# Chain outputs turned by VectorE, and small transfers issued by GpSimd, in a hybrid layer

## The chip, the cores and the metric

The kernel runs on one core of a Trainium2 chip. The engines of that core are TensorE (PE, matrix products and transposes; PEld is its weight load), VectorE (DVE), ScalarE (ACT), GpSimd (POOL) and SyncE (SP); 16 DMA engines move data between memory and the core. An engine that issues a transfer does so in its own instruction queue. The metric is the device time of one execution in microseconds (us), taken as the median of several runs.

## The reference

One layer of a decoder trunk on `x` of 1024 tokens by 1024 channels, in float32. The input projection feeds two mixers, whose outputs are concatenated and projected back; then comes a gated MLP with a short convolution. Cut to what matters:

```python
h = rmsnorm(x, norm1_w)
proj = h @ w_in
# mixer A: 4 heads of 128, chunked delta rule
o_a = gated_delta_rule(qa, ka, va, g, beta)
o_a = rmsnorm(o_a, gdn_norm_w) * silu(z)
# mixer B: 8 heads of 64, three dilated windows merged by their denominators
num_tot = wts[0] * nums[0] + wts[1] * nums[1] + wts[2] * nums[2]
den_tot = wts[0] * dens[0] + wts[1] * dens[1] + wts[2] * dens[2]
o_b = num_tot / den_tot
x = x + concatenate([o_a, o_b]) @ w_out
u = causal_dwconv(rmsnorm(x, norm2_w) @ w_up, ffn_conv_w)
x = x + (silu(u[..., :D_FF]) * u[..., D_FF:]) @ w_down
out = rmsnorm(x, final_norm_w)
```

## The kernel before

Activations are kept channel-major (128 channels by 1024 tokens a tile). A float32 product is three passes over high and low halves (`xhi`·`whi`, `xlo`·`whi`, `xhi`·`wlo`), called a product of three passes here. The input projection runs column by column in the order of the list `DENSE`: the last key column, the values of the attention, the q and v columns of the delta-rule heads, eight attention columns `a`, and four gate columns `z`. Weights are fetched two columns ahead by `take`; for the last twelve columns (`a`, `z`) ScalarE makes the high half `whi` and GpSimd the low half `wlo` (L225).

The delta rule of head h is `chain(h)`: eight chunks of 128 tokens, one after the other. Heads 0 and 1 run ahead of heads 2 and 3. At its end GpSimd takes a power (`ms`) and scales the token-major output `vtok` by it, and `finish(h, vtok)` (L926) turns that output to channel-major. Heads 0 and 1 are turned by TensorE (`tp`, eight transposes each), copied with the factor `gw2` by ScalarE to a tile `ot`, and written by SP to `mixer`. Heads 2 and 3 are turned by VectorE, whose transpose works inside blocks of 32 by 32, and the blocks are put in place by eight writes to `odram`, 512 runs of 32 numbers each. A gate column `z` reads the head's output back as `og` (one transfer from `mixer`, or four from `odram`) and multiplies it with the gate.

The attention begins when the outputs of all four heads are written (`wv.until(("o", h))`). It takes eight groups (four pairs of heads, two halves of the tokens). In a group, each pair of blocks goes through `scores`, `softmax`, `turn` (TensorE transposes the weights, VectorE and ScalarE copy them to `pt` and `pb`), and `values`; `merge_classes` adds the dilated part. For groups 0 to 6 `rows_out` brings the reciprocals of the denominators across partitions: VectorE turns them (`dt`), four transfers of 1 KB write them to `ddram`, two transfers read them, repeated over 64 partitions, as `rT`. `give` (L1101) multiplies the accumulator with `rT` to `oT`, and frees one of two accumulator banks. `ot`, `rT` and `oT` share a ring `t2` of two buffers. The factors of the second norm take a similar way in `rms2_power`: four writes to `ndram` and one read, `rstdB`.

The order of TensorE's work is set by a planner (`Weave`) that runs the parts of the program as streams with priorities and keeps an estimate of each engine's time; the order it finds is fixed for TensorE by a token (`mm` L194, `tp` L198). The other engines' order is made by a scheduler after that, and each executes its queue in order. The object that issues is an `Engine` (L142, L144); `sy` and `sq` are two names of SP's queue with different costs for the planner, and `sq` issues the small transfers: the writes `odram`, the reads `og` from it, `ddram`, `rT` and `ndram`.

Of the kernel before, what the change touches and what calls it, by code (L numbers as in the profile page):

```python
# [7 lines left out]
F32 = mybir.dt.float32  # L8
F32R = mybir.dt.float32r
AF = mybir.ActivationFunctionType  # L10
OP = mybir.AluOpType
# [4 lines left out]
P = 128  # L16
# [3 lines left out]
NCH = 8  # L20
# [127 lines left out]
def hybrid_layer(tc, I, out):  # L148
    nc = tc.nc
    wv = Weave()  # L150
    ve = Engine(wv, nc.vector, "vector", 0.07, 0.00105)
    ac = Engine(wv, nc.scalar, "scalar", 0.12, 0.00085)
# [2 lines left out]
    ua = Engine(wv, nc.scalar, "scalar", 0.12, 0.00085, first=tc.high_priority)  # L155
    po_ = Engine(wv, nc.gpsimd, "gpsimd", 0.15, 0.0021)
    sy = Engine(wv, nc.sync, "sync", 0.05, 0.00142, 2.2)
    sq = Engine(wv, nc.sync, "small", 0.05, 0.00036, 0.4)
    sa = Engine(wv, nc.scalar, "actq", 0.05, 0.00142, 2.2)
    es = ExitStack()  # L160
    cp = es.enter_context(tc.tile_pool(name="cp", bufs=1))
# [2 lines left out]
    sp = es.enter_context(tc.tile_pool(name="sp", bufs=1))  # L164
# [3 lines left out]
    def tile_(pool, shape, dt, name, tag, bufs):  # L168
        return wv.slot(pool.tile(list(shape), dt, name=name, tag=tag, bufs=bufs), tag, bufs)
# [3 lines left out]
    def A(name, tag, dt=F32, shape=(P, 1024)):  # L173
        if tag in TURNS:
            i = turns[tag] = turns.get(tag, -1) + 1
            tag = TURNS[tag][i % len(TURNS[tag])]
        return tile_(lp, shape, dt, name, tag, SLOTS[tag])
# [4 lines left out]
    def const(name, shape, src=None):  # L182
        t = cp.tile(list(shape), F32, name=name)
        if src is not None:
            sy.dma_start(t, src)
        return t
# [10 lines left out]
    def tp(dst, src, idt=None, us=0.11):  # L197
        tc.stamp_issue_order_token(nc.tensor.transpose(dst, src, ident if idt is None else idt).ins, TOKEN)  # L198
        wv.product(us, dst, src)
# [13 lines left out]
    def raw_weight(src, n=1024):  # L213
        st = tile_(wp, [P, n], F32, "wst", "wst", 2)
        sy.dma_start(st, src)
        return st
# [37 lines left out]
    mixer = dp.tile([8, P, S], F32, name="mixer")  # L254
# [10 lines left out]
    odram = dp.tile([H, 32, 4 * S], F32, name="odram")  # L265
# [3 lines left out]
    def bank(tag, name="ps"):  # L269
        return tile_(pp_, (P, 512), F32, name, tag, 2)  # L270

    def next_bank(tag, *tiles, slack=0.0):

        while max(wv.need(*tiles), wv.slot_free(tag, 2)) + slack > 1e-3:
            yield max(wv.need(*tiles), wv.slot_free(tag, 2)) + slack
        return bank(tag)

    def half(i):
        return slice(i * 512, i * 512 + 512)

    def v8(t):
        return t.rearrange("p (c t) -> p c t", c=NCH)
# [83 lines left out]
    gw2 = const("gw2", [P, 1])  # L366
# [149 lines left out]
    def silu2(xr, name):  # L516
        y = A(name, "ev")
        ac.activation(y, xr, AF.Tanh, scale=0.5)
        ve.scalar_tensor_tensor(y, y, 1.0, xr, op0=OP.add, op1=OP.mult)
        return y  # L520
# [8 lines left out]
    def first_keys():  # L529
        xr = [scaled(pst[2 * h:2 * h + 2], "xr", tag=("ev", "ev", "qa")[h]) for h in range(3)]  # L530
        for h in range(3):
            T["k", h] = conv_silu(xr[h], 4 + h, "kT", "kT*")
            wv.add(3, kprep(h))
            yield wv.need(T["k", h])

    def dense():

        yield from wv.until("first")
        yield from wv.until("norms")
        wv.add(2, first_keys())  # L540

        srcs, tiles = [], 0
        for col in DENSE:
            if col[0] == "V":
                srcs += [I["wv"][j] for j in range(4)]
            else:
                srcs.append(I["wi"][tiles])
                tiles += 1
        place = [0]
        raw = [raw_weight(srcs[0])]  # L550
        nxt = [weight(None, st=raw.pop())]
        raw.append(raw_weight(srcs[1]))

        def take():
            w = nxt.pop()
            i = place[0] = place[0] + 1
            if i < len(srcs):
                nxt.append(weight(None, st=raw.pop(), spare=i >= 17))
            if i + 1 < len(srcs):
                raw.append(raw_weight(srcs[i + 1]))  # L560
            return w

        def values_by_token(g):

            banks = [bank(t) for t in ("asc", "asc", "ch", "ch")]
            for j in range(4):
                w = [t.rearrange("p (k m) -> p k m", k=2) for t in take()]
                for kk in range(2):
                    k = 2 * j + kk
                    for i, pt in enumerate(banks):  # L570
                        c = 4 * g + i
                        yield wv.need(pt, *w)
                        mm3(pt, [t[:, c * P:(c + 1) * P] for t in xs[k]], [t[:, kk, :] for t in w], k == 0, k == KT - 1)
            for i in range(0, 4, 2):
                vx = A("vx", "ev", shape=(P, 2, 512))
                for e in range(2):
                    c = 4 * g + i + e
                    ac.activation(vx[:, e, :], banks[i + e], AF.Copy, scale=rst[:, c:c + 1])
                c = 4 * g + i
                sy.dma_start(vpark[c * P:(c + 2) * P].rearrange("(e p) d -> p e d", e=2), vx)  # L580
            wv.done.add(("V", g))

        for i, col in enumerate(DENSE):
            kind, h = col[:2]
            if kind == "V":
                yield from values_by_token(h)
                continue
            if kind == "z":
                yield from wv.until(("o", h))
            w = [t.rearrange("p (k m) -> p k m", k=KT) for t in take()]  # L590
            pair = []
            for hh in range(2):
                pt = bank("hf")
                yield wv.need(pt, *w)
                for k in range(KT):
                    mm3(pt, [t[:, k, :] for t in w], [t[:, half(hh)] for t in xs[k]], k == 0, k == KT - 1)
                    yield 0.0

                pair.append(pt)
                if hh == 0:  # L600
                    xr = A("aqkv" if kind == "a" else "xr", "go" if kind == "k" else "ev")
                scaled(pair, "xr", kind == "a", t=xr, hs=(hh,))
            if kind == "k":
                T["k", h] = conv_silu(xr, 4 + h, "kT", "kT*")
                wv.add(3, kprep(h))
            elif kind == "q":
                q = conv_silu(xr, h, "qT", "qa")
                wv.add(4, qprep(h, q))
            elif kind == "v":
                v = conv_silu(xr, 8 + h, "vT", "qa")  # L610
                wv.add(4, vprep(h, v))
            elif kind == "z":
                og = gated[h] = A("og", "kT*")
                if h > 1:
                    of = odram[h].rearrange("j (c a t) -> a j c t", c=NCH, a=4)
                    for a in range(4):
                        sq.dma_start(v8(og)[32 * a:32 * a + 32], of[a])
                else:
                    sy.dma_start(og, mixer[h])
                zz = silu2(xr, "zz")  # L620
                if h > 1:
                    ve.scalar_tensor_tensor(og, og, gw2, zz, op0=OP.mult, op1=OP.mult)
                else:
                    ve.tensor_tensor(og, og, zz, op=OP.mult)
            else:
                sy.dma_start(apark[h, col[2]], xr)
                wv.done.add(col)
        wv.done.add("dense")
# [295 lines left out]
        wv.add(1, finish(h, vtok))  # L924

    def finish(h, osb):  # L926
        if h > 1:
            yield wv.need(osb)
            for hh in range(2):
                ot = tile_(sp, [P, 512], F32, "ot", "t2", 2)  # L930
                for c in range(4):
                    ve.transpose(ot[:, c * P:c * P + P], osb[:, (4 * hh + c) * P:(4 * hh + c + 1) * P])
                to = odram[h].rearrange("j (f b i) -> b j f i", f=32, b=4)[:, :, 16 * hh:16 * hh + 16]
                for b in range(4):
                    sq.dma_start(to[b], ot[32 * b:32 * b + 32].rearrange("p (f i) -> p f i", i=32))
        for hh in range(2 * (h < 2)):
            pt = yield from next_bank("atr", osb)
            for c in range(4):
                i = 4 * hh + c
                tp(pt[:, c * P:(c + 1) * P], osb[:, i * P:(i + 1) * P])  # L940
            ot = tile_(sp, [P, 512], F32, "ot", "t2", 2)
            ac.activation(ot, pt, AF.Copy, scale=gw2)
            sy.dma_start(mixer[h][:, half(hh)], ot)
        wv.done.add(("o", h))


# [797 lines left out]
```

## Time and profile before

| what | us |
| --- | --- |
| median of 3 runs | 1196.23 (1195.36 to 1197.35) |
| the profiled execution, its time | 1197.55 |
| the profiled execution, its span | 1195.7 |
| TensorE busy in it | 1182.3 |
| VectorE busy | 918.3 |
| ScalarE busy | 569.5 |
| GpSimd busy | 81.5 |

The clock granted to TensorE was 0.998 of full speed over the span. All rows quoted from the profile come from the one profiled execution, and their times count from the start of its span. A row of a timeline gives start, duration, engine, line, operation, output and inputs, and in brackets how long the engine stood idle before it and what ended that. L142, L144, L194 and L198 are lines of helpers, so that rows are told apart by the names of tiles.

### The profile page before, as it was taken

To read this page: it belongs to the slowest core of one execution; us is meant where nothing else is said; L and a number is where in the kernel's file an instruction comes from. 1 tells how busy PE (TensorE), PEld (TensorE's weight loads), DVE (VectorE), ACT (ScalarE), POOL (GpSimd) and SP (SyncE) were. 2 spreads that over 40 slices of the span, in tenths; PEclk is the share of its full clock that TensorE was granted. 3 is DMA by queue.
4 is the path that set the end of the run, shared out by engine and by line. 5 is a ranking of instruction groups with operands and counts; after the bars stand their busy time and mean duration, and the time that the engine had idled before them with its cause. 6 is when DMAs were issued, how large, how long until landed. Compare 5 with 4: busy or idle time off the path is not lost.

```text
span 1195.7 us, 18260 instructions
## 1 busy us (share of the span) xinstructions
PE 1182.3 (99%) x6998; PEld 977.3 (82%) x6998; DVE 918.3 (77%) x1473; ACT 569.5 (48%) x1115; POOL 81.5 (7%) x74
## 2 busy tenths in 40 slices
PE   9999999999999999999999999999999999999997
PEld 7888888888777778888888888888888888887886
DVE  7673975666365665777898898989889889998875
ACT  7275345355354533555554444445444453434441
POOL 0212010214211110000000000000000000000000
PEclk9999999999999999999999999999999999999999
DMA  7334234435944214443322313132231397546514
GB/s 244 101 95 150 80 116 127 143 122 172 220 147 129 86 52 135 159 159 106 106 86 73 106 53 106 54 106 81 78 103 56 127 368 284 197 160 211 168 53 141
DMA packets 100023, 157.20 MB, mean 131 GB/s; under 512 B 30400, under 2 KB 51168, under 8 KB 99936
## 3 DMA queue, kind: packets, MB, share of 16 engines
q1 hardware_dynamic: 99072, 155.25, 40.1%
q8 instruction: 55, 0.90, 0.3%
q10 hardware_dynamic: 864, 0.79, 0.2%
q14 instruction: 32, 0.26, 0.1%
HBM read 120.04 MB, written 35.96 MB: 130 GB/s over the span
## 4 chain that ended last, share of the span: by engine, by line
PE 93%; DVE 3%; ACT 2%; issue 1%; DMA 1%; POOLq 0%; POOL 0%; DVEq 0%; SPq 0%; ACTq 0%
PE ps L194 45%; PE pa L194 20%; PE dw L194 15%; PE pc L194 10%; PE ps L198 2%; DVE kT L142 1%; DMA wd<-in_wd 1%; DVE x1h L142 0%; ACT sm L144 0%; DVE pr L142 0%; DMA xt<-in_xT 0%; ACT whi L142 0%; DVE zz L142 0%; DVE wd L142 0%; ACT dec L142 0%
## 5 line engine op out<-in xcount | busy, mean ns | idle before, releaser
L194 PE MATMUL dw<-pr 128*128 128x512 f32 (+1 forms) x984 | 212.0, 377 | 0.3 <-DVE x1h L142 0.2
L194 PEld LDWEIGHTS dw<-pr 128*128 128x128 f32 x984 | 176.6, 188 | 34.7 <-DVE x1h L142 1.2
L194 PE MATMUL ps<-xhi,whi 128*128 128x512 f32 x384 | 157.1, 409 | 0.1
L194 PE MATMUL ps<-xhi,wlo 128*128 128x512 f32 x384 | 150.1, 391 | 0.0
L194 PE MATMUL ps<-xlo,whi 128*128 128x512 f32 x384 | 148.3, 390 | 0.0
L194 PE MATMUL pa<-T,pair 128*128 128x512 f32 x528 | 127.1, 389 | 0.1
L194 PEld LDWEIGHTS pa<-T,pair 128*128 128x128 f32 x528 | 99.0, 188 | 20.9 <-ACT u L142 0.5
L194 PEld LDWEIGHTS ps<-xhi,whi 128*128 128x128 f32 x384 | 72.3, 188 | 19.1 <-issue 5.6
L194 PEld LDWEIGHTS ps<-xhi,wlo 128*128 128x128 f32 x384 | 72.2, 188 | 15.6
L194 PEld LDWEIGHTS ps<-xlo,whi 128*128 128x128 f32 x384 | 72.3, 188 | 12.6
L142 ACT ACTIVATE u<-pa 128x512 f32<-128x512 f32 x44 | 26.3, 598 | 108.7 <-PE pa L194 108.7
L142 DVE SCALAR_TENSOR_TENSOR y<-xu,fcw,y 128x1023 f32<-128x1023 f32 (+1 forms) x44 | 56.4, 1281 | 23.3 <-ACT y L142 23.2
L142 ACT ACTIVATE whi<-wst 128x1024 fp32r<-128x1024 f32 x36 | 38.2, 1065 | 63.6 <-PE ps L194 45.9
L194 PE MATMUL pa<-B,A 128*128 128x512 f32 x264 | 63.4, 389 | 0.0
L194 PE MATMUL pc<-T,S 128*128 128x512 f32 x264 | 63.4, 389 | 0.0
L194 PE MATMUL pa<-T,S 128*128 128x512 f32 x264 | 63.4, 389 | 0.0
L194 PE MATMUL pc<-B,pair 128*128 128x512 f32 x264 | 63.4, 389 | 0.0
L142 ACT ACTIVATE pr<-r 128x1024 fp32r<-128x1024 f32 (+1 forms) x44 | 36.6, 840 | 51.8 <-PE dw L194 29.5
L142 DVE TENSOR_TENSOR wst<-wst 128x512 f32<-128x512 f32 x88 | 60.4, 687 | 0.8
L194 PE MATMUL ps<-B,pair 128*128 128x512 f32 x252 | 60.5, 389 | 0.0
L194 PEld LDWEIGHTS pa<-T,S 128*128 128x128 f32 x264 | 49.6, 188 | 10.3
L194 PEld LDWEIGHTS pc<-B,pair 128*128 128x128 f32 x264 | 49.6, 188 | 10.3
(255 smaller groups left out, 2322.5 us busy)
## 6 DMA issues: line engine op xcount, KB each, us to landing
wst<-in_wu SPq DMA_DIRECT2D x44, 512.0 KB
wd<-in_wd SPq DMA_DIRECT2D x44, 512.0 KB
upark<-y SPq DMA_DIRECT2D x22, 512.0 KB
wst<-in_wi SPq DMA_DIRECT2D x21, 512.0 KB
r<-upark SPq DMA_DIRECT2D x11, 512.0 KB
r<-upark SPq DMA_DIRECT2D x22, 256.0 KB
wa<-in_wd SPq DMA_DIRECT2D x22, 256.0 KB
wst<-in_wv SPq DMA_DIRECT2D x8, 512.0 KB
```

The lines of the kernel that those rows point to most:

```text
L142: return getattr(eng, op)(*a, **kw)
L194: tc.stamp_issue_order_token(nc.tensor.matmul(dst, lhs, rhs, start=start, stop=stop, **kw).ins, TOKEN)
L198: tc.stamp_issue_order_token(nc.tensor.transpose(dst, src, ident if idt is None else idt).ins, TOKEN)
```

## The change

The name `sq` now stands for GpSimd's queue. `finish` does one thing for all heads: its stream waits until the planner has placed the last chunks of chains 2 and 3, then VectorE turns the output and eight transfers of `sq` write it to `odram`. The gate columns read every head by four transfers of `sq` and always apply `gw2`.

```diff
-    sq = Engine(wv, nc.sync, "small", 0.05, 0.00036, 0.4)
+    sq = Engine(wv, nc.gpsimd, "small", 0.05, 0.00036, 0.4)
...
             elif kind == "z":
                 og = gated[h] = A("og", "kT*")
-                if h > 1:
-                    of = odram[h].rearrange("j (c a t) -> a j c t", c=NCH, a=4)
-                    for a in range(4):
-                        sq.dma_start(v8(og)[32 * a:32 * a + 32], of[a])
-                else:
-                    sy.dma_start(og, mixer[h])
-                zz = silu2(xr, "zz")
-                if h > 1:
-                    ve.scalar_tensor_tensor(og, og, gw2, zz, op0=OP.mult, op1=OP.mult)
-                else:
-                    ve.tensor_tensor(og, og, zz, op=OP.mult)
+                of = odram[h].rearrange("j (c a t) -> a j c t", c=NCH, a=4)
+                for a in range(4):
+                    sq.dma_start(v8(og)[32 * a:32 * a + 32], of[a])
+                ve.scalar_tensor_tensor(og, og, gw2, silu2(xr, "zz"), op0=OP.mult, op1=OP.mult)
...
     def finish(h, osb):
-        if h > 1:
-            yield wv.need(osb)
-            for hh in range(2):
-                ot = tile_(sp, [P, 512], F32, "ot", "t2", 2)
-                for c in range(4):
-                    ve.transpose(ot[:, c * P:c * P + P], osb[:, (4 * hh + c) * P:(4 * hh + c + 1) * P])
-                to = odram[h].rearrange("j (f b i) -> b j f i", f=32, b=4)[:, :, 16 * hh:16 * hh + 16]
-                for b in range(4):
-                    sq.dma_start(to[b], ot[32 * b:32 * b + 32].rearrange("p (f i) -> p f i", i=32))
-        for hh in range(2 * (h < 2)):
-            pt = yield from next_bank("atr", osb)
+        for i in (2, 3):
+            yield from wv.until(("c", i, NCH - 1))
+        yield wv.need(osb)
+        for hh in range(2):
+            yield 0.3
+            ot = tile_(sp, [P, 512], F32, "ot", "t2", 2)
             for c in range(4):
-                i = 4 * hh + c
-                tp(pt[:, c * P:(c + 1) * P], osb[:, i * P:(i + 1) * P])
-            ot = tile_(sp, [P, 512], F32, "ot", "t2", 2)
-            ac.activation(ot, pt, AF.Copy, scale=gw2)
-            sy.dma_start(mixer[h][:, half(hh)], ot)
+                ve.transpose(ot[:, c * P:c * P + P], osb[:, (4 * hh + c) * P:(4 * hh + c + 1) * P])
+            to = odram[h].rearrange("j (f b i) -> b j f i", f=32, b=4)[:, :, 16 * hh:16 * hh + 16]
+            for b in range(4):
+                sq.dma_start(to[b], ot[32 * b:32 * b + 32].rearrange("p (f i) -> p f i", i=32))
         wv.done.add(("o", h))
```

Three places show how the order of instructions moves. The first is TensorE among the last chunks of the chains: the difference from before (-) to after (+), where head 0 was turned. `xhi`, `wlo` belong to the input projection; `wke`, `ktok`, `r`, `um` to the chains.

```order
 L194 MATMUL ps<-xlo,whi 128x512
 L194 MATMUL ps<-xhi,wlo 128x512
-L198 MATMUL ps<-ident,vtok 128x128 x8
-L194 MATMUL ps<-wke,ktok 128x128
-L194 MATMUL ps<-r,um 128x128
```

The eight transposes of head 0 are gone (and two times four of head 1, a little later); products of the projection and the chains are interleaved anew around that place. Of the products of three passes that stood ahead of the turn of attention group 4, four now stand earlier, ahead of group 2.

The second place is GpSimd from the end of chain 0 on, difference from before to after. `ms` is the power at the end of a chain, `vtok` the scaled output, `pb` a cleared tile of the attention.

```order
 L142 TENSOR_TENSOR ms<-ms,mhalf 128x8
+L142 DMA odram<-ot 32x16x32
 L142 TENSOR_TENSOR vtok<-vtok,ms 128x1024
+L142 DMA odram<-ot 32x16x32 x7
 L142 MEMSET pb 32x2x128
 L142 TENSOR_TENSOR ms<-ms,mhalf 128x8
+L142 TENSOR_TENSOR wlo<-wst,whi 128x1024
 L142 TENSOR_TENSOR vtok<-vtok,ms 128x1024
-L142 TENSOR_TENSOR wlo<-wst,whi 128x1024
+L142 DMA odram<-ot 32x16x32 x8
 L142 MEMSET pb 32x2x128
```

The writes of heads 0 and 1 now stand between the powers, the scaled outputs and the low halves of GpSimd's own work. Further down the same queue after the change, from the small writes of attention group 1 to the reads of group 2:

```order
 L142 DMA ddram<-dt 8x32 x4
 L142 DMA rT<-ddram 64x4x128 x2
 L142 DMA og<-odram 32x8x128 x3
 L142 MEMSET pb 32x2x128 x2
 L142 DMA og<-odram 32x8x128
 L142 DMA ddram<-dt 8x32 x4
 L142 DMA rT<-ddram 64x4x128 x4
```

Here the reads for groups 0, 1 and 2 stand behind the chain writes of all heads and among the reads `og`.

The third place is VectorE where the accumulator of attention group 0 is given out (`oT` with the factors `rT`). Before, that stands behind the copies of group 1's first pair:

```order
L144 COPY pt_3530<-ps_3531 128x4x64
L144 COPY pb_3408<-ps_3531 96x2x64
L144 COPY pt_3530<-ps_3550 128x4x64
L144 COPY pb_3408<-ps_3550 128x2x64
L142 TENSOR_TENSOR oT_3690<-ps_3424,rT_3470 128x4x4x32
L144 ISA sm_3601,mx_3602<-ps_3585,mk_2954 128x416
```

After, it stands behind the denominators (`dt`) and copies of group 2:

```order
L142 STREAM_TRANSPOSE dt_3921<-dn_2956 128x32
L144 COPY pt_3879<-ps_3880 128x4x64
L144 COPY pb_3637<-ps_3880 32x2x64
L144 COPY pt_3879<-ps_3899 128x4x64
L144 COPY pb_3637<-ps_3899 64x2x64
L142 TENSOR_TENSOR oT_3715<-ps_3443,rT_3489 128x4x4x32
L144 ISA sm_3952,mx_3953<-ps_3936,mk_2954 128x352
```

So the product with `rT` of group 0 moved past the whole second half of group 1 and the first pairs of group 2.

## The prediction

> **What bounds the kernel now.** I read the page's first and fourth parts first, to see which engine holds the end:
>
> ```profile
> PE 1182.3 (99%) x6998; PEld 977.3 (82%) x6998; DVE 918.3 (77%) x1473; ACT 569.5 (48%) x1115; POOL 81.5 (7%) x74
> ...
> PE 93%; DVE 3%; ACT 2%; issue 1%; DMA 1%; POOLq 0%; POOL 0%; DVEq 0%; SPq 0%; ACTq 0%
> ```
>
> TensorE is the bound. An edit pays only by removing TensorE work or its waits, and costs only where TensorE is made to wait. Next, busy time by stage, where the edits lie: the last chains (240 to 311 us), the reads of chain outputs (311 to 330), the attention's first groups (330 to 357). Columns: stretch, its length, busy time of each engine (instructions), granted clock, DMA share, GB/s.
>
> ```profile
> 240.00:311.00 71.00, 69.97 (x457) 62.65 (x456) 42.23 (x134) 37.09 (x139) 21.30 (x16) 1.00 0.54 157
> 311.00:330.00 19.00, 17.74 (x144) 13.15 (x142) 7.58 (x31) 7.11 (x21) 3.86 (x2) 1.00 0.93 230
> 330.00:357.00 27.00, 27.00 (x378) 20.85 (x376) 17.01 (x63) 13.95 (x50) 3.27 (x4) 1.00 0.49 142
> sum 117.00, PE 114.71 PEld 96.65 DVE 66.82 ACT 58.15 POOL 28.44; mean PE 38.24 PEld 32.22 DVE 22.27 ACT 19.38 POOL 9.48
> ```
>
> TensorE idles 117.00 − 114.71 = 2.29 us in all of it, so there is little to win beyond removed work. Its waits between 240 and 480 us are as small:
>
> ```profile
> PE ps L198 <- ACT sm L144: 1.7, 4, 1.1
> PE ps L194 <- ACT w L144: 0.5, 1, 0.5
> PE ps L194 <- DVE ct L144: 0.4, 1, 0.4
> ```
>
> None of them is for a small transfer: SP's issue is hidden today.
>
> **Part 1, the turn of heads 0 and 1 leaves TensorE: −1.75 us.** From the timeline of TensorE (start, duration), the first eight transposes and what follows them, then two consecutive products:
>
> ```profile
> 284.65 1.03 PE L198 MATMUL ps<-ident,vtok 128*128 128x128 f32 x8
> 285.52 0.39 PE L194 MATMUL ps<-wke,ktok 128*128 128x128 f32 x2
> ...
> 387.28 0.39 PE L194 MATMUL ps<-xhi,whi 128*128 128x512 f32 x1
> ...
> 387.96 0.39 PE L194 MATMUL ps<-xhi,whi 128*128 128x512 f32 x1
> ```
>
> Eight take 285.52 − 284.65 = 0.87 us, so 16 give 1.75 us back. The second pair of rows prices a product of three passes: 387.96 − 387.28 = 0.68 us. The order moves four of these from ahead of the turn of group 4 (380 to 390 us) to earlier places: 4 × 0.68 = 2.7 us of TensorE work now precede group 2's merge. That adds nothing to the sum, but moves a due time, below.
>
> **Part 2, what VectorE and ScalarE gain and lose: 0.**
>
> ```profile
> L142 DVE STREAM_TRANSPOSE ot<-vtok x16: 268/269/314, 296.9 to 311.6; 128x128 f32<-128x128 f32 x16
> ...
> L142 ACT ACTIVATE ot<-ps,gw x4: 682/688/689, 285.3 to 290.5; 128x512 f32<-128x512 f32 x4
> ```
>
> Sixteen more transposes are 16 × 0.269 = 4.3 us of VectorE; ScalarE loses 4 × 0.688 = 2.8 us. The cover is VectorE's free time, 117.00 − 66.82 = 50 us. Without it they would cost up to 4.3 us. The factor `gw2` moves into one VectorE instruction that replaces another of the same shape, for the z columns: 0.
>
> **Part 3, the small transfers move to GpSimd's queue: the term that decides.** What GpSimd does there today (grouped by line from 281 to 372 us: count, busy, mean ns), and where the queue starts:
>
> ```profile
> L142 POOL TENSOR_TENSOR wlo<-wst,whi 128x1024 fp32r<-128x1024 f32 x5 | 11.9, 2376 | 22.6 <-ACT whi L142 22.6
> L142 POOL TENSOR_TENSOR vtok<-vtok,ms 128x1024 f32<-128x1024 f32 x4 | 7.6, 1898 | 0.3
> L142 POOL TENSOR_TENSOR ms<-ms,mhalf 128x8 f32<-128x8 f32 x4 | 6.5, 1637 | 12.3 <-DVE ms L142 12.2
> L142 POOL MEMSET pb<- 32x256 f32 x7 | 2.1, 304 | 40.7 <-PE ps L194 34.8 <-issue 5.8
> ...
> 283.77 1.64 POOL L142 TENSOR_TENSOR ms<-ms,mhalf 128x8 f32<-128x8 f32 x1
> ```
>
> In the new order the first write of a chain output stands right behind the power of head 1, which ends at 283.77 + 1.64 = 285.41 us. From there to the two reads `rT` of attention group 2 the queue holds 66 transfers (32 `odram` writes, 16 `og` and 6 `rT` reads, 12 `ddram` writes), and between them GpSimd's own work: 3 norms, 2 powers, 4 low halves, 5 clearings = 3 × 1.90 + 2 × 1.64 + 4 × 2.38 + 5 × 0.30 = 20.0 us.
>
> What GpSimd takes to issue one transfer stands in no row. The nearest rows from below are SP's for the same transfers (minimum/median/maximum in ns):
>
> ```profile
> L142 SPq DMA_DIRECT2D odram<-ot x16: 303/502/1822, 298.2 to 316.4; - x16
> L142 SPq DMA_DIRECT2D og<-odram x8: 551/605/955, 305.7 to 320.6; - x8
> ...
> L142 SPq DMA_DIRECT2D rT<-ddram x14: 579/613/629, 331.7 to 420.3; - x14
> ...
> L142 SPq DMA_DIRECT2D ddram<-dt x28: 269/288/458, 329.5 to 418.4; - x28
> ```
>
> Lower end: 32 × 0.50 + 16 × 0.605 + 6 × 0.61 + 12 × 0.29 = 33 us. Upper end: GpSimd's dearest row, 2.38 us, for each of the 54 larger transfers and its clearing, 0.30 us, for the small ones: 54 × 2.38 + 12 × 0.30 = 132 us. I take a value between, from the same engine's rate: 2376 ns over 1024 columns = 2.32 ns per contiguous piece to be addressed, on top of 0.30 us. A chain write has 512 pieces of 32 numbers: 1.49 us; a read of 256 pieces 0.89 us; a small write 0.32 us. Sum: 32 × 1.49 + 22 × 0.89 + 12 × 0.32 = 71.1 us. I choose by that row because it is the same engine, and SP's are not.
>
> [...] The trace of before holds no transfer of GpSimd to compare.
>
> So the queue comes to the end of `rT` of group 2 at 285.41 + 20.0 + 71.1 = 376.5 us. When is it due? First row: SP's issue of group 2's `rT`; then VectorE around it.
>
> ```profile
> 358.79 1.27 SPq L142 DMA_DIRECT2D rT<-ddram  x2
> ...
> 356.32 0.21 DVE L142 STREAM_TRANSPOSE dt<-dn 128x32 f32<-128x32 f32 x1
> ...
> 357.68 0.27 DVE L144 COPY pb<-ps 64x128 f32<-64x128 f32 x1
> ...
> 365.09 1.09 DVE L142 TENSOR_TENSOR oT<-ps,rT 128x512 f32<-128x512 f32 x1 [0.88 <-PE ps L194]
> ```
>
> The four writes ahead of that issue end at 357.85 and it begins 0.94 us later, which is the landing; I add 1.0, so the factors are there at 377.5 us. `oT` of group 2 needs them at 365.09 − 1.75 (transposes gone) + 2.7 (products placed earlier) = 366.05. VectorE waits 11.45 us. Behind that instruction stand, in its order, the softmax maxima of group 3, for which TensorE waits after some five products; these cover the softmax itself, as they do now, so the wait passes to TensorE whole. As a formula, with S for the 66 transfers: wait = S − 59.65 if positive, total = S − 61.4; with S = 71.1, −1.75 + 11.45 = **+9.7 us**.
>
> Two earlier due times of the same queue are contained in that, not added. The low half of attention column 5, made by GpSimd behind 16 chain writes, and the product that first reads it:
>
> ```profile
> 310.09 2.40 POOL L142 TENSOR_TENSOR wlo<-wst,whi 128x1024 fp32r<-128x1024 f32 x1
> ...
> 320.63 0.40 PE L194 MATMUL ps<-xhi,wlo 128*128 128x512 f32 x1
> ```
>
> It would be ready at 285.41 + 12.4 (2 norms, 2 powers, 2 low halves, 2 clearings) + 16 × 1.49 = 321.7 against 320.63 − 1.75: some 3 us of wait already there. And `oT` of group 0, which the new order puts behind group 2's copies (they end at 357.95), has its factors only some 9.0 us ahead of group 2's (4 reads `og`, 4 reads `rT`, 4 small writes and 2 clearings stand between: 8 × 0.89 + 4 × 0.32 + 2 × 0.30), near 368: VectorE stands from 358 on. After group 2 the queue is through: `dt` to `oT` leaves 365.09 − 356.32 = 8.8 us, and four writes, two reads and two landings take 4 × 0.32 + 2 × 0.89 + 2 = 5.1. A low half between them adds 2.4 and fits.
>
> The extra chain traffic (16 writes of 512 pieces) meets engines already full:
>
> ```profile
> q1 hardware_dynamic: 12978, 7.35, 92.5%
> ```
>
> That is packets, MB and share from 298 to 330 us: 0.925 × 32 × 16 / 12978 = 36 ns a packet at most, and 8192 more are 18.7 us of all 16 engines. Spread by the slow queue over 90 us, of which 330 to 357 is half free, they cost 0; issued at SP's pace they would delay weights that are fetched two columns ahead, which cover them.
>
> The second norm's factors: VectorE today waits 1.07 us for them,
>
> ```profile
> 572.12 1.23 DVE L142 TENSOR_TENSOR xu<-xu,rstdB 128x1024 f32<-128x1024 f32 x1 [1.07 <-DMA rstdB<-ndram]
> ```
>
> and four writes by GpSimd may add 4 × (0.32 − 0.29) up to 4 × 2 = 8 us; I take 0, as the queue is empty by then and TensorE's rows there do not wait.
>
> **Sum.** The profiled execution took 1197.55 us (span 1195.7), 1.3 above the median of 1196.23. 1197.55 + 9.7 = 1207.3; against the median 1205.9, rounded to 1206.
>
> **Rivals.**
> *The queue is cheap.* With S below 59.65 nothing waits: 1196.2 − 1.75 = 1194.5. For it: SP's rows give 33, and none of today's waits is for small transfers. Against it: SP's rows are another engine's. This is the case on the other side, and it decides from S = 59.65, a mean of 0.9 us a transfer. Chance 0.24.
> *The queue is as slow as GpSimd's dearest row.* S = 132, total +70.6: 1266.8. For it: the row of the low halves is the same engine over 1024 columns; against it: a chain write has half as many pieces. Chance 0.10.
> *VectorE holds GpSimd up.* [...] Against it: GpSimd's low half at 310.09 took 2.40 us, as its mean of 2.38, whatever VectorE did. Chance 0.06. [...]
> *The new place of group 0's `oT` costs.* With a cheap queue it is still given at 357.95, done at 359.04, and frees the accumulator bank that group 2's values take:
>
> ```profile
> 357.08 0.88 PE L194 MATMUL ps<-pt,vn 128*64 128x128 f32 x12
> ```
>
> That is a wait of up to 359.04 − 357.08 = 2.0 us: +0.2, 1196.4. Chance 0.10.
>
> **How the numbers follow.** The forecast keeps 0.50. A measurement of this kernel tells 0.2% (2.4 us) from no change. Faster: 0.14 of the cheap queue (a little more than the transposes is won) and 0.03 of the last rival, 0.17. Same: the cheap queue's other 0.10, 0.05 of the last rival and 0.03 of the forecast (S from 59 to 63.8), 0.18. Slower: the rest, 0.65. The forecast's own range, with a chain write between 1.2 and 2.2 us, is S from 62 to 94, 1197 to 1229. The range reaches from the cheap queue (1194) to the dear one (1267) and leaves out only part of the first and the hold-up by VectorE.
>
> **What would show it.** Right: no `ident,vtok` rows; chain writes on GpSimd near 1.5 us each; TensorE idle of some 11 us between 315 and 380, released by a low half and by `sm`, with VectorE's `oT` waiting for `rT`; nothing after 400 us. Wrong: chain writes under 1 us each and no such idle (cheap), or an idle of tens of us (dear), or idle at 560 to 580 us (norm factors).

## The result, and the profile after

The changed kernel takes 1202.59 us (median of 6 runs, 1199.75 to 1204.29); the kernel before, run beside it, takes 1196.42 us. The ratio is 1.0042, 95% interval 1.0030 to 1.0053: 0.4% slower, +6.2 us where +9.7 was forecast. The profiled execution took 1202.77 us with a span of 1201.0, 5.3 more than before.

GpSimd's part of the change is priced by the transfers that it now issues (tile view; minimum/median/maximum in ns, then the first and last start):

```profile
L142 POOL DMA_DIRECT2D odram<-ot x32: 648/648/912, 285.5 to 336.7; - x32
L142 POOL DMA_DIRECT2D og<-odram x16: 582/582/603, 315.5 to 352.7; - x16
```
```profile
L142 POOL DMA_DIRECT2D rT<-ddram x14: 615/636/668, 347.4 to 428.6; - x14
```
```profile
L142 POOL DMA_DIRECT2D ddram<-dt x28: 497/516/538, 332.7 to 425.0; - x28
```

The forecast had 1.49, 0.89, 0.89 and 0.32 us. With these medians its S is 32 × 0.648 + 16 × 0.582 + 6 × 0.636 + 12 × 0.516 = 40.1 us instead of 71.1, below the 59.65 from which the queue was to make anyone wait. By its own formula the change should have gained 1.75 us. The loss has other places. TensorE's waits between 240 and 480 us (what it waited for; us in total, times, longest):

```profile
PE ps L198 <- ACT sm L144: 2.0, 7, 0.6
PE ps L194 <- DVE dn L144: 1.9, 1, 1.9
PE ps L194 <- DVE oT L142: 1.8, 1, 1.8
```

Two are new. The first stands in the timelines of GpSimd, VectorE and TensorE around 358 us:

```profile
347.36 1.29 POOL L142 DMA_DIRECT2D rT<-ddram  x2
...
357.87 0.27 DVE L144 COPY pb<-ps 64x128 f32<-64x128 f32 x1
358.07 1.03 DVE L142 TENSOR_TENSOR oT<-ps,rT 128x512 f32<-128x512 f32 x1
...
359.16 0.88 PE L194 MATMUL ps<-pt,vn 128*64 128x128 f32 x12 [1.82 <-DVE oT L142]
```

The factors of group 0 are issued by 348.65 us. Their product `oT` starts only at 358.07, and right behind a copy, without idle time: it waited for its place in VectorE's order, not for data. TensorE waits 1.82 us for the accumulator bank that it frees. The second wait is one for data (SP, GpSimd, VectorE and TensorE):

```profile
377.89 0.32 SPq L142 DMA_DIRECT2D qT<-apark  x1
378.30 0.38 SPq L142 DMA_DIRECT2D wst<-in_wi  x1
382.38 1.80 SPq L142 DMA_DIRECT2D vn<-vpark  x4
384.27 1.20 SPq L142 DMA_DIRECT2D vc<-vpark  x2
...
377.05 2.02 POOL L142 DMA_DIRECT2D ddram<-dt  x4
383.43 1.28 POOL L142 DMA_DIRECT2D rT<-ddram  x2 [4.37 <-DMA ddram<-dt]
...
376.15 0.21 DVE L142 STREAM_TRANSPOSE dt<-dn 128x32 f32<-128x32 f32 x1
...
389.87 1.06 DVE L142 TENSOR_TENSOR oT<-ps,rT 128x512 f32<-128x512 f32 x1 [8.11 <-DMA rT<-ddram]
...
393.46 0.50 PE L194 MATMUL ps<-xhi,whi 128*128 128x512 f32 x1 [1.88 <-DVE dn L144]
```

From the end of `dt` at 376.36 us to `oT` pass 13.5 us. The four small writes of group 3 are issued by 379.07 us, and GpSimd waits 4.37 us for their landing before it can issue the reads; SP had issued two large reads (`qT` and weights, `wst`) from 377.89 on. The reads `rT` are issued by 384.71 us and land some 5 us later; SP's reads `vn` and `vc` are issued around them, from 382.38 to 385.47. So both halves of the way are late, each beside large reads of SP. From 382 to 391 us SP's queue took 57.6% of the 16 DMA engines' time and GpSimd's 13.3%. That this load is the reason fits, but is not shown apart. VectorE stands 8.11 us, and TensorE 1.88 us for the softmax behind it. After each of the two waits TensorE runs on at a lower granted clock (the column after the five busy times):

```profile
360.00:363.00 3.00, 3.00 (x44) 1.86 (x43) 1.03 (x5) 0.41 (x1) 0.67 (x2) 0.61 0.54 178
363.00:366.00 3.00, 3.00 (x12) 2.13 (x10) 1.96 (x7) 2.04 (x8) 0.00 (x0) 0.82 0.00 0
...
395.00:400.00 5.00, 5.00 (x68) 3.71 (x64) 2.07 (x7) 1.30 (x5) 4.75 (x6) 0.68 0.35 120
```

That is 3 × 0.39 + 3 × 0.18 = 1.7 us and 5 × 0.32 = 1.6 us, as much again as the waits. The profile's account up to the last attention group: −1.75 (transposes) + 1.82 + 1.7 + 1.88 + 1.6 + 0.8 (two smaller waits for `sm`, 0.58 and 0.19) = +6.0 us. The first `rd` copy, which stands in that group, moved by 431.2 − 424.7 = 6.5 us:

```profile
L142 POOL COPY rd<-mx x4: 290/292/293, 424.7 to 432.9; 128x128 f32<-128x128 f32 x4
```
```profile
L142 POOL COPY rd<-mx x4: 288/290/292, 431.2 to 439.4; 128x128 f32<-128x128 f32 x4
```

(first before, then after). Why the spans differ by 1.2 us less than that stays open.

### The profile page after: what moved, and what is told of

Its sections match the earlier page's. It is cut to its first block, busy times and chain, and to the rows that moved or that the text cites. A ratio compares the mean times of both kernels' runs of the same rounds, so it can differ in the third digit from the quotient of the medians.

```text
span 1201.0 us, 18272 instructions
## 1 busy us (share of the span) xinstructions
PE 1183.7 (99%) x6982; PEld 977.3 (81%) x6982; DVE 920.2 (77%) x1489; ACT 566.7 (47%) x1111; POOL 137.0 (11%) x168
## 3 DMA queue, kind: packets, MB, share of 16 engines
q1 hardware_dynamic: 83264, 149.18, 38.2%
q0 software_dynamic: 3488, 6.07, 2.4%
## 4 chain that ended last, share of the span: by engine, by line
PE 91%; DVE 3%; DMA 2%; ACT 2%; issue 1%; POOL 1%; SPq 0%; POOLq 0%; DVEq 0%; ACTq 0%
PE ps L194 42%; PE pa L194 20%; PE dw L194 17%; PE pc L194 10%; PE ps L198 2%; DVE kT L142 1%; ACT sm L144 1%; DMA rT<-ddram 0%; DMA vc<-vpark 0%; DVE sm L144 0%; DMA ddram<-dt 0%; DMA xt<-in_xT 0%; DVE og L142 0%; DVE aqkv L142 0%; DVE x1h L142 0%
## 5 line engine op out<-in xcount | busy, mean ns | idle before, releaser
L142 POOL TENSOR_TENSOR rs<-rs,mhalf 128x2 f32<-128x2 f32 (+2 forms) x4 | 4.5, 1133 | 735.3 <-DVE rs L144 735.3
L144 ACT ACTIVATE sm<-sm,mx 128x128 f32<-128x128 f32 (+7 forms) x64 | 35.5, 555 | 54.3 <-DVE mx L144 54.3
```

Of the source, the lines that this page charges most:

```text
L142: return getattr(eng, op)(*a, **kw)
L144: return getattr(eng, op)(*a, **kw)
```

## The experiments

These theories were put to the runs. **Q**, the forecast: the time GpSimd takes to issue decides. **V**: the turn by VectorE itself costs, whichever queue writes its outputs. **L**: `oT` of group 0 in its late place, and `rT` of group 3 landing late beside SP's large reads, each with a low clock behind it. **C**, formed after the first four runs: the 32 chain writes and 16 reads `og` crowd one stretch, and the attention's first `rT` comes behind them in whichever queue; **P** is its rival, that the extra transfers cost wherever they stand. Ratios are to runs of the kernel before on the same chip, with 95% intervals; edits are against the changed kernel unless said otherwise.

**The two halves of the change apart.** All small transfers back on SP:

```diff
-    sq = Engine(wv, nc.gpsimd, "small", 0.05, 0.00036, 0.4)
+    sq = Engine(wv, nc.sync, "small", 0.05, 0.00036, 0.4)
```

> All small transfers go back to SP's queue, everything else as after the change; TensorE's order is that of after, and VectorE gives group 0's oT out at its old place again. Theory L (two late places: oT of group 0 behind group 2's copies, and the landing of rT of group 3 behind SP's large reads, each followed by a lower granted clock): both waits go, only the 16 transposes stay saved: 1196.4 - 1.75 = 1194.7 us, no single TensorE wait over 1 us between 330 and 420 us. Theory Q (the forecast: the price of GpSimd's queue): also 1194.7. Theory V (the turn on VectorE itself, with TensorE's new order and 16 more chain writes, costs): stays above 1198 us.

Measured: 1200.95 us, ratio 1.0029 (1.0017 to 1.0041). Neither Q nor L, but V at this point: with no transfer on GpSimd most of the loss is still there. Its profile has both late places of L gone and another wait instead. SP, VectorE and TensorE:

```profile
318.89 7.76 SPq L142 DMA_DIRECT2D odram<-ot  x8
...
333.81 3.57 SPq L142 DMA_DIRECT2D ddram<-dt  x4
340.15 1.29 SPq L142 DMA_DIRECT2D rT<-ddram  x2
...
344.48 1.06 DVE L142 TENSOR_TENSOR oT<-ps,rT 128x512 f32<-128x512 f32 x1 [8.43 <-DMA rT<-ddram]
...
346.85 1.32 PE L198 MATMUL ps<-ident,sm 64*128 64x64 f32 x16 [4.55 <-ACT sm L144]
```

Eight chain writes take 7.76 us to issue, close to 1 us each instead of 0.50 at the median, and the reads `og` follow; group 0's four small writes come at 333.81 (329.48 before) and its `rT` at 340.15 (331.70 before). The granted clock from 330 to 357 us was 0.87.

The other half: the kernel before with `sq` on GpSimd, nothing else.

```diff
-    sq = Engine(wv, nc.sync, "small", 0.05, 0.00036, 0.4)
+    sq = Engine(wv, nc.gpsimd, "small", 0.05, 0.00036, 0.4)
```

> The turn and the gate columns as before, only the small transfers go to GpSimd: 16 chain writes, 8 og reads and the attention's small ones. VectorE gives group 0's oT out ahead of group 1's denominators. L: the accumulator bank is free in time, so no wait near 357 us; the rT reads can still land late beside SP's large reads: 0 to 2 us of wait and as much again by the clock, 1196.4 to 1200. Q: half of the queue's chain work is gone, its 24 fewer transfers take 24 x 0.63 = 15 us out, and nothing is late: 1196.4. V: 1196.4.

Measured: 1198.68 us, ratio 1.0012 (1.0003 to 1.0022), within the range that L gave (1196.4 to 1200); Q and V gave 1196.4. VectorE's `oT` waited 10.4 us for `rT` in two places, TensorE 0.60 us at the longest of it. So the turn costs 0.29%, the queue 0.12%, and both together 0.42%. The figures add up, but TensorE's waits behind them do not: the wait of 4.55 us with all on SP is not in the changed kernel, and the two of the changed kernel are not in either half.

**Which transfers.** The attention's and the norm's back on SP, the chain's on GpSimd (`ss` is a second name of SP's queue, as in the next run):

```diff
-    sq = Engine(wv, nc.gpsimd, "small", 0.05, 0.00036, 0.4)
+    sq, ss = [Engine(wv, q, "small", 0.05, 0.00036, 0.4) for q in (nc.gpsimd, nc.sync)]
...
-                    sq.dma_start(to[:, 32 * b:32 * b + 32], dt[32 * b:32 * b + 8, :])
+                    ss.dma_start(to[:, 32 * b:32 * b + 32], dt[32 * b:32 * b + 8, :])
...
-                    sq.dma_start(rT[er].rearrange("p (u t) -> p u t", u=4),
+                    ss.dma_start(rT[er].rearrange("p (u t) -> p u t", u=4),
```

> As after, but the attention's and the norm's small transfers (ddram, rT, ndram) go by SP; the 32 chain writes and 16 og reads stay on GpSimd. L: oT of group 0 stands ahead of group 2's denominators and rT goes ahead of the large reads in SP's own queue: both waits go, 1194.7 us (up to 1196 if what is left of the delay of oT costs something). Q: 48 of the 66 transfers stay on GpSimd, and most of the loss stays: above 1198.

Measured: 1200.09 us, ratio 1.0022 (1.0012 to 1.0033). TensorE's waits at L's two places are gone from the profile, but group 1's `oT` waits 3.15 us for `rT` and TensorE 2.63 us at 359.60, with a clock of 0.95 from 357 to 390 us. The time agrees with Q's figure, not its reason: the wait is for `rT`, which SP issued here. And the opposite split (`ss` for `odram` and `og` instead):

> As after, but the chain writes and og reads go by SP; ddram, rT and ndram stay on GpSimd. VectorE's order is that of the kernel with all on SP. L: the bank wait near 357 us goes (1.8 us and about 1.7 by the clock); rT of group 3 still lands beside SP's large reads and VectorE waits for it: 1194.7 + 0 to 3.5 = 1194.7 to 1198.2. Q: 18 of 66 transfers are left, nothing is late: 1194.7.

Measured: 1207.24 us, ratio 1.0083 (1.0063 to 1.0103), the slowest of all but the tripled writes below, where both theories had it among the fastest. TensorE waits 7.8 us for `sm`, in eleven places. What ended VectorE's idle time ahead of `oT` (us, times):

```profile
  DMA rT<-ddram: 19.0, 4
  DMA vc<-vpark: 7.4, 1
```

GpSimd is occupied for 9.4 of the 27.0 us from 330 to 357 here; yet it takes 3.7 to 7.0 us, in the first four groups, from the issue of four small writes to that of their read, which waits for their landing beside what SP issued. That the DMA engines' load is the reason is argued, not shown apart. This is the end of Q: with 18 of the 66 transfers on GpSimd instead of all, the loss is twice that of the changed kernel.

**The late place alone, on the kernel before.** `given[0]` is group 0's `oT`; it is ordered behind VectorE's copies of group 2's second pair:

```diff
-                        copy(it["pb"][i][:rows, :, u, rr], pv[:rows, :, nn + i, :])
+                        last = copy(it["pb"][i][:rows, :, u, rr], pv[:rows, :, nn + i, :])
+                    if it["g"]["n"] == 2 and u == 3 and rr == HALVES[0]:
+                        after(given[0], last)
...
-            ve.tensor_tensor(oT.rearrange("p (n u c) -> p n c u", n=4, c=4), *by, op=OP.mult)
+            given.append(ve.tensor_tensor(oT.rearrange("p (n u c) -> p n c u", n=4, c=4), *by, op=OP.mult))
```

> The kernel before, with one change: VectorE's oT of group 0 is held until its copies of group 2's second pair, the place it has after the change. Theory L (the place makes TensorE wait for the accumulator bank, and the granted clock falls after the idle): one wait of 1.8 us near 358 us, and 1.7 us by a granted clock near 0.7 for 5 us behind it: 1196.8 + 3.5 = 1200.3. If idle costs no clock: 1198.6. If the place costs nothing: 1196.8.

Measured: 1201.72 us, ratio 1.0038 (1.0025 to 1.0051): +4.5 us for one instruction in another place. TensorE's wait is the one of the changed kernel to the hundredth, and the clock falls behind it:

```profile
359.79 0.88 PE L194 MATMUL ps<-pt,vn 128*64 128x128 f32 x12 [1.82 <-DVE oT L142]
```
```profile
357.00:360.00 3.00, 1.18 (x29) 1.03 (x30) 2.42 (x7) 0.96 (x4) 0.00 (x0) 1.00 0.12 31
360.00:366.00 6.00, 6.00 (x62) 4.21 (x59) 2.10 (x6) 0.57 (x2) 0.00 (x0) 0.72 0.30 99
```

1.82 + 6 × 0.28 = 3.5 us, as expected. The rest is within the interval (3.0 to 6.1 us).

**What puts it there.** The ring of `ot`, `rT` and `oT` with three buffers (every `"t2", 2` becomes `"t2", 3`; the room comes from three small tiles used at the start):

```diff
-            ot = tile_(sp, [P, 512], F32, "ot", "t2", 2)
+            ot = tile_(sp, [P, 512], F32, "ot", "t2", 3)
...
-                rT = g["rT"] = tile_(sp, [P, 512], F32, "rT", "t2", 2)
+                rT = g["rT"] = tile_(sp, [P, 512], F32, "rT", "t2", 3)
...
-            oT = tile_(sp, [P, 512], F32, "oT", "t2", 2)
+            oT = tile_(sp, [P, 512], F32, "oT", "t2", 3)
```

> As after, but the ring that ot, rT and oT share has three buffers instead of two (room is made by sharing three small tiles that are used at the start). TensorE's order differs from after in little. The ring theory (rT of group 0 has to wait for the landing of head 3's writes because it takes their buffer, so oT of group 0 is placed late): oT of group 0 stands ahead of group 2's denominators, the bank wait of 1.8 us and its clock go, 1202.6 - 3.5 = 1199. If the ring doesn't matter and the queue's order does: as after, 1202.

Measured: 1198.88 us, ratio 1.0011 (1.0002 to 1.0020), the expected 1199. `oT` of group 0 starts at 350.6 us, and no wait of TensorE is over 0.6 us. So the ring of two buffers takes part in the late place. In the changed kernel GpSimd also stands 6.3 us ahead of two later reads `rT` until an `oT` is through; with three buffers no read waits for that. How the ring leads to the late place is less sure: `rT` of group 0 stands behind head 3's last writes in both kernels, but with two buffers (347.36 us) also behind a low half and group 1's small writes, with three (343.05 us) ahead of them. That the scheduler waits there for the landing of head 3's writes, whose buffers `rT` takes, is an inference from the code. Not holding heads 0 and 1 back is another way to get `oT` to its earlier place (350.7 us):

```diff
-        for i in (2, 3):
-            yield from wv.until(("c", i, NCH - 1))
         yield wv.need(osb)
```

> As after, but heads 0 and 1 are turned as soon as their chains end; the planner's wait for chains 2 and 3 is taken out, TensorE's order differs from after in ten lines only. Theory C (crowding: 32 chain writes and 16 og reads are issued in one stretch from 300 to 337 us, and the attention's first rT stands behind them in whichever queue): 16 of the writes are done before 300 us, oT of group 0 stands ahead of group 2's denominators, and the bank wait of 1.8 us with its clock goes; rT of group 3 may still land late (up to 3.5 us): 1195 to 1199. Theory P (the 16 more writes and the four more reads cost wherever they stand): as after, 1202.

Measured: 1200.62 us, ratio 1.0034 (1.0015 to 1.0054). The profiled execution, of 1196.1 us span, has no wait over 0.72 us, yet ten runs lie from 1197.8 to 1207.8 us. The granted clock was 0.994 to 0.995 in the three runs over 1205 us and 0.997 to 0.998 in the three under 1200 us; what those longer runs waited for is not in a profile, and C is left undecided by this one. With the transfers on SP:

> The same with all small transfers on SP: the difference to the kernel with all on SP is only that heads 0 and 1 are not held. C: its wait of 4.5 us before the transposes near 347 us and the low clock after it shrink by most: 1195 to 1197. P: as with all on SP, 1201.

Measured: 1199.34 us (1194.96 to 1202.33), ratio 1.0014 (1.0003 to 1.0025) against 1.0029 with the heads held back. The profile shows what C says, the small writes of group 0 at 330.67 us and no wait of TensorE for `sm` over 0.2:

```profile
PE ps L194 <- ACT w L144: 1.2, 2, 0.7
PE ps L194 <- DVE ct L144: 0.7, 2, 0.5
PE ps L198 <- ACT sm L144: 0.4, 2, 0.2
```

That execution's span is 1193.2 us, 2.5 under before's, TensorE is busy 1180.3 us instead of 1182.3, and the first `rd` copy starts at 423.2 us instead of 424.7: the transposes' 1.75 us are there to be had. But it is the shortest of ten runs, and the median stays 0.14% above the kernel before. It lies between C's 1195 to 1197 and P's 1201, and the intervals of this run and of the one held back overlap, so that C is not shown.

**The second wait.** Only group 3's six small transfers go by SP; TensorE's and VectorE's orders stay word for word:

```diff
-                    sq.dma_start(to[:, 32 * b:32 * b + 32], dt[32 * b:32 * b + 8, :])
+                    (ss if g["n"] == 3 else sq).dma_start(to[:, 32 * b:32 * b + 32], dt[32 * b:32 * b + 8, :])
...
-                    sq.dma_start(rT[er].rearrange("p (u t) -> p u t", u=4),
+                    (ss if g["n"] == 3 else sq).dma_start(rT[er].rearrange("p (u t) -> p u t", u=4),
```

> As after, but group 3's six small transfers (four ddram, two rT) go by SP, where rT stands ahead of the reads vn and vc. TensorE's and VectorE's orders are those of after, word for word. Theory L (rT of group 3 lands 5 us after its issue because SP's reads vn and vc share the DMA engines with it, so VectorE's oT waits 8.1 us and TensorE 1.9, and the clock falls): the second wait, near 392 us, and the low clock of 395 to 400 us go, the first wait at 357 us stays: 1202.6 - 1.9 - 1.6 = 1199.1. If the queue that issues doesn't matter: 1202.

Measured: 1202.55 us, ratio 1.0047 (1.0030 to 1.0064): a miss. In the profile the step does what L says, `oT` of group 3 waits 3.08 instead of 8.11 us and TensorE's wait near 392 us is gone, as is the low clock there; the span is 1.4 us shorter. In exchange group 2's `oT` waits 3.36 us for `rT`, and TensorE 1.14 us at 376.68, where it was 0.58 in the changed kernel. The median is not shorter. The wait at 393 us stands in one execution of the changed kernel; how often it comes is open, and so is what it costs the median.

**More of the queue.** Each chain write issued three times:

```diff
-                sq.dma_start(to[b], ot[32 * b:32 * b + 32].rearrange("p (f i) -> p f i", i=32))
+                for _ in range(3):
+                    sq.dma_start(to[b], ot[32 * b:32 * b + 32].rearrange("p (f i) -> p f i", i=32))
```

> As after, but each of the 32 chain writes is issued three times (the same data to the same place), so that GpSimd's 66 transfers become 130. By the issue times of the profile after (0.65 us a chain write) S goes from 40 to 81.5 us. The forecast's formula (total = S - 61.4 when S is over 59.65): +20 us, 1217. If the queue had slack enough all the same: as after, 1202 to 1205. The 64 more writes also load the DMA engines, which can add to either.

Measured: 1228.46 us (two runs), ratio 1.026 (1.0239 to 1.028): +31 us. At S = 81.5 the longer queue makes TensorE wait, as the forecast's formula said of such an S, but in other places. TensorE's longest waits (beside one of 3.62 at 378.54):

```profile
341.98 0.97 PE L198 MATMUL ps<-ident,sm 64*128 64x64 f32 x8 [6.02 <-ACT sm L144]
...
413.57 1.55 PE L194 MATMUL ps<-pt,vn 128*64 128x128 f32 x12 [7.50 <-DVE oT L142]
```

Ahead of the first, VectorE stood 3.64 us until earlier writes had landed and freed a buffer `ot`; the second is `oT` of group 0, whose `rT` GpSimd issues only at 408.52 us, behind the chain writes. The forecast had priced the factors of group 2 alone. The formula gave +20; from 285 to 420 us TensorE is idle 18.1 us, and the clock, for which the formula has no term, is 0.91 on the mean (135 × 0.09 = 12 us). So a longer queue can decide, and the changed kernel is below that; where the threshold lies, and what the 64 more writes cost the DMA engines, is not shown.

**A version meant to beat both.** Heads not held back, ring of three, all on SP:

> VectorE turns all heads, with nothing held, all small transfers on SP, and the ring of ot, rT and oT with three buffers. Theories L and C: no late rT and no late oT is left, the 16 transposes are saved: 1197.2 - 1.75 = 1195.4, at best 1194. If the 16 more chain writes cost in any place: above 1197.

Measured: 1199.49 us, ratio 1.0017 (1.0008 to 1.0026): a miss for L and C, on the side on which the 16 more chain writes cost. Group 0's small writes are issued at 333.66 us, as late as with the heads held back (333.81), although nothing is held, and TensorE waits twice for `sm`, 1.13 and 1.14 us, at 345 and 347 us. And with the chain writes and `og` on GpSimd:

> VectorE turns all heads, nothing is held, the chain writes and og reads go by GpSimd (few packets, own queue), the attention's and the norm's small transfers by SP (ahead of SP's large reads), and the ring of ot, rT and oT has three buffers. If lateness of rT is all that the change costs: every oT stands at its old place and waits for TensorE alone, no single TensorE wait over 1.2 us between 240 and 480 us, 16 transposes saved: 1197.3 - 1.75 = 1195.5 us. If the turn by VectorE costs something beyond that: 1197 or more.

Measured: 1198.23 us (1195.23 to 1200.27), ratio 1.0002 (0.9988 to 1.0016), the best version with the turn by VectorE, no better than the kernel before. The condition of the expected 1195.5, no late `rT`, was not met: VectorE's `oT` still waited 9.2 us for `rT` in two places, and TensorE 2.04 us at 358.18, a little more than the transposes give back. So with that split no cost of the turn is left to show (V in its plain form is not borne out), and no variant was shown to do better than the kernel before.

## Why the prediction was right, and where it was wrong

The direction, the size within a factor of two and the range (1194 to 1267) came out. The reason did not: by the prediction's own signs (chain writes under 1 us, no idle of some 11 us) this is the case of its rival "the queue is cheap", and the time that this rival gave, 1194.5, did not come either.

- *Part 1, −1.75 us*: the rows of the 16 transposes are gone, and TensorE's busy time in the shortest profile with the new turn (1180.3 instead of 1182.3 us) shows the gain. It holds as work; no variant's median shows it as time.
- *Part 2, VectorE's and ScalarE's work at 0*: nothing speaks against it; TensorE's new waits are for places and data, not for VectorE's load.
- *Part 3, the price of a GpSimd transfer*: the step that failed. The forecast scaled GpSimd's arithmetic rate to pieces (1.49 us a chain write); it measured 0.648 for 512 pieces and 0.582 for 256. In these rows the number of pieces hardly enters. SP's rows, the lower bound, were the better guide. S was 40.1, not 71.1, and the wait of 11.45 us for a backlog did not come.
- *The low half of column 5* was done by 310.51 + 2.39 = 312.9 us, not 321.7. No wait there, as the price was wrong.
- *The 16 more writes at 0, "fetched two columns ahead, which cover them"*: failed where SP issues them. The weights were covered, but not the attention's first factors, which stand behind those writes. Without GpSimd this half costs +0.29% instead of gaining 0.15%.
- *After group 2 the queue is through*: failed for group 3. The sum took 1 us for a landing; the small writes took 4.37 us and the reads about 5, and `dt` to `oT` 13.5 us instead of the 8.8 there was time for. Over all groups a read `rT` landed 2.9 us after its issue began at the least, 3.5 at the median.
- *The norm's factors at 0*: held; VectorE's `xu` at 579.88 starts without idle time.
- *The rival "the new place of group 0's `oT` costs"*: this is what happened first. It had the place and the wait (up to 2.0 us; measured 1.82), a chance of 0.10 and a result of +0.2, because it left out the clock behind the idle (1.7 us) and the late data of a later group.
- *The rival "VectorE holds GpSimd up"*: no issue of a chain write took over 0.912 us, and the median equals the minimum (0.648 us), although VectorE was busy for 26.2 of the 51.9 us in which these writes were issued (285.5 to 337.4 us). A chain write landed 2.7 us after its issue began, at the median.

So the sign was luck, an accident of two errors: one wait was priced at 11.45 us and did not come, and several that were priced at nothing or next to it did.

## What to carry to other kernels

When transfers change queue, ask first what they share with others, namely buffers of a ring (in the changed kernel GpSimd stood 6.3 us ahead of two reads `rT` until an `oT` was through), DMA engines (late landings beside SP's reads, the cause not shown apart) and a place in an in-order queue (`oT` of group 0 started 9.4 us after its factors were issued), and only then what an issue costs. A product that frees an accumulator bank should be followed through the scheduler's new order, and its wait priced with the lower clock that may follow it; here 1.82 us of waiting were followed by some 6 us at 0.72, another 1.7 us, which doubled the price. Moving only a part of the small transfers to another queue can be worse than moving all of them (here 0.83% against 0.42%).

## What the runs showed of the hardware

- An idle time of TensorE of 1.82 us, right behind 0.9 us of transposes, was followed in two kernels by some 6 us at a mean granted clock of 0.72, and one of 1.88 us, right behind products, by 5 us at 0.68 (from 395 us on).
- In the changed kernel GpSimd issued a write of 512 pieces in 0.648 us at the median and one of 8 in 0.516: 64 times the pieces took 0.13 us more. SP's issue of the writes of 512 pieces ranged from 0.30 to 2.17 us in the kernel with all on SP.
- The same transfers made far fewer packets from GpSimd (queue, packets, MB, share of 16 engines; first the kernel with all small transfers on SP, then the changed one):

```profile
q1 hardware_dynamic: 108832, 155.25, 40.9%
```
```profile
q1 hardware_dynamic: 83264, 149.18, 38.2%
q0 software_dynamic: 3488, 6.07, 2.4%
```

  From SP these 6.07 MB took 108832 − 83264 = 25568 packets. In 3488 packets they are 1.7 KB each, although most of those transfers consist of pieces of 128 or 512 bytes.
